# Four token rows of a PEER layer, copied eight times in HBM before they are given out to 128 partitions

## The chip, the cores and the metric

The kernel runs on one core of a Trainium2 chip. The metric is the time of one execution on the device in microseconds (us). A core has a matrix engine (TensorE, PE in the profile, with its weight loads as PEld), a vector engine (VectorE, DVE), a scalar engine (ScalarE, ACT), a general engine (GpSimd, POOL) and an engine that mostly issues DMAs (SyncE, SP). Sixteen DMA engines move data between the chip's memory (HBM) and the on-chip memory (SBUF, 128 partitions), whichever engine issues the transfer.

## The reference

One decoder layer on 256 tokens of width 2048, in float32: two kinds of attention, a normalization, a PEER layer, a normalization, a gated embedding, a normalization. The change lies in the PEER layer, which looks up 8 x 16 = 128 experts of 16384 for each token, and adds up their outputs:

```python
def block(args):
    xb, eb, gb = args              # tokens, chosen experts, gates
    ub = u[eb]                     # rows of peer_u, 2048 wide
    vbk = v[eb]                    # rows of peer_v
    act = jax.nn.gelu(jnp.einsum('thed,td->the', ub, xb).astype(jnp.float32))
    w = (gb * act).astype(xb.dtype)
    return jnp.einsum('the,thed->td', w, vbk)
```

`peer_u` and `peer_v` have 16384 rows of 8 KB, 134 MB each.

## The kernel before

**Stages.** Attention and the first normalization fill the first 415 us or so. Then follow the query (16 blocks of `peer_wq`, function `query`), 128 blocks of `peer_u` (`u_block`), 256 half blocks of `peer_v` (`v_block`), and the second normalization with the gate. Blocks of weights are loaded by SP with `su.load` (line 97) into `wf`, which has `WF = 5` buffers; a load is issued when PE has finished with the buffer.

**Two ways to the same sum.** The last 156 tokens (`NDT`) are computed densely: all 16384 activations by matmuls against the whole of `peer_u` (line 206, results through ACT in line 942, one activation per block), multiplied by gates that are zero but for the chosen experts (`gate_work`, whose small matmuls are lines 903 and 904 and whose scaling on DVE is line 913), then matmuls against `peer_v` (line 992). The first 100 tokens (`NSP`) are computed sparsely, by the function `sparse_work`: the rows of their chosen experts are gathered from HBM, 128 at a time, one for each partition, by an indirect DMA that POOL issues (line 851); DVE multiplies each gathered row by its token's x and sums (line 824); later the same goes for `peer_v`.

**Groups of tokens.** The sparse tokens are in three groups, `GROUPS = ((0, 64), (64, 32), (96, 4))`. The 128 partitions are shared out among the tokens of a group: in the first group each token has 2 partitions and 64 gathers are needed, in the second 4 partitions and 32 gathers, in the third 32 partitions and 4 gathers. So each partition needs the x of its token, and this is the tile `xq{i}`, a megabyte, made by the function `tokens` (line 803). It reads the tokens' rows of `s_x1` from HBM, repeated by an access pattern with a step of zero: 64 rows each twice, 32 rows each four times, 4 rows each 32 times. The first two are issued when `sparse_work` starts, the third (`xq2`) at the ninth gather of the second group. It takes over the buffer of `xq0`.

**Where x comes from.** The tensor `s_x1` is in HBM. In the query stage a background job, `spill_x1`, applies the last step of the normalization to x on POOL (lines 576 and 577) and writes it there in two DMAs of a megabyte (line 586), the first for tokens 0 to 127.

**Order.** SP, POOL and ACT each issue their DMAs in program order. The gathers are spread out: `gathers(n)` lets n of them out per block (1.8 per query block, 0.7 per block of `peer_u`, 0.35 per half block of `peer_v`), and each is held on POOL by a little copy (`pace`, line 849) until a 4-byte DMA on SP's queue (`mark`, line 848) has landed behind the loads before it. Four buffers (`NGB`) hold gathered rows. `keep` marks instructions that the scheduler leaves in program order.

Of the kernel before, what the change touches and what calls it, by code (L numbers as in the profile page):

```python
# [9 lines left out]
F32 = mybir.dt.float32  # L10
# [9 lines left out]
P = 128  # L20
T = 256
NT = T // P
D = 2048
# [16 lines left out]
SEG2 = NIA - SEG1  # L40

GROUPS = ((0, 64), (64, 32), (96, 4))
NSP = sum(n for _, n in GROUPS)
NDT = T - NSP
SELB = 8
# [110 lines left out]
def build(tc, a, out):  # L156
    nc = tc.nc
# [286 lines left out]
    x1 = [x1p.tile([P, D], F32, name=f"x1_{t}") for t in range(NT)]  # L444
# [68 lines left out]
    def ln_rows(pool, which):  # L513
        gr = pool.tile([P, D], F32, name="g_row", tag="g_row")
        br = pool.tile([P, D], F32, name="b_row", tag="b_row")
        load(gr, a["ln_g"][which:which + 1, :].to_broadcast([P, D]))
        load(br, a["ln_b"][which:which + 1, :].to_broadcast([P, D]))
        return gr, br
# [55 lines left out]
    def affine(xt, c, gr, br):  # L574
        s = slice(c * 512, (c + 1) * 512)
        nc.gpsimd.tensor_tensor(xt[:, s], xt[:, s], gr[:, s], op=ALU.mult)
        nc.gpsimd.tensor_tensor(xt[:, s], xt[:, s], br[:, s], op=ALU.add)

    def spill_x1():
        gr, br = ln_rows(rowp, 0)  # L580
        yield 4
        for t in range(NT):
            for c in range(NCH):
                affine(x1[t], c, gr, br)
                yield 10 if t else 4
            nc.gpsimd.dma_start(a["s_x1"][t * P:(t + 1) * P, :], x1[t])


    gin = pools.open("gin", "left", bufs=1)
# [8 lines left out]
    sel, eig, eact, ew = [], [], [], []  # L598
    for i, (_, n) in enumerate(GROUPS):
        sel.append(gin.tile([P, n], F32, name=f"sel{i}"))  # L600
# [98 lines left out]
    def gates(t):  # L699
# [12 lines left out]
        if t == 0:  # L712
            nc.vector.tensor_copy(eg[:NSP, 1].bitcast(F32), g[:NSP])
            for i in range(len(GROUPS)):
                slots(i, 1, by_slot(i, 1))
# [5 lines left out]
    def slots(i, w, src):  # L721

        t0, n = GROUPS[i]
        nc.gpsimd.dma_start(eig[i][:, w],
                            src[t0:t0 + n].rearrange("t (r j) -> t r j", j=n))

    def by_slot(i, w):

        t0, n = GROUPS[i]
        src = eg[t0:t0 + n, w].bitcast(F32)  # L730
        if n < PH:
            return eg[:, w].rearrange("t h k -> t (h k)")
        dst = es[t0:t0 + n, w].bitcast(F32)
        nc.vector.tensor_copy(dst.rearrange("t (r h c) -> t h r c", h=PH, r=P // n),
                              src.rearrange("t h (r c) -> t h r c", r=P // n))
        return es[:, w]

    def head_slots(h):

        c = slice(h * TOPK, (h + 1) * TOPK)  # L740
        nc.vector.scalar_tensor_tensor(eg[:NSP, 0, h], iaN[:NSP, 0, c], float(NKEY),
                                       ibN[:NSP, 0, c], op0=ALU.mult, op1=ALU.add)
        t0, n = GROUPS[0]
        m = n // PH
# [50 lines left out]
    def sparse_work():  # L795


        xq = []

        def tokens(i):  # L800
            t0, n = GROUPS[i]
            xq.append(gin.tile([P, D], F32, name=f"xq{i}", tag=f"xq{i % 2}"))
            nc.gpsimd.dma_start(xq[i], a["s_x1"][t0:t0 + n, None, :].to_broadcast([n, P // n, D]))

        tokens(0)
        tokens(1)
        made = []

        dots, acts = [], []

        def advance():

            if acts and gated:
                i, b = acts.pop(0)
                keep(nc.vector.tensor_tensor(ew[i][:, b], ew[i][:, b],
                                             eig[i][:, 1, b].bitcast(F32), op=ALU.mult))
            if dots:
                i, b = dots.pop(0)
                keep(nc.scalar.activation(ew[i][:, b], eact[i][:, b], AF.Gelu_apprx_tanh))
                acts.append((i, b))  # L820

        def use(kind, i, j, g):
            if kind == "u_rows":
                keep(nc.vector.scalar_tensor_tensor(g, g, 1.0, xq[i], op0=ALU.mult, op1=ALU.mult,  # L824
                                                    accum_out=eact[i][:, j:j + 1]))
            elif j == 0:
                if i < 2:
                    ys[i] = gin.tile([P, D], F32, name=f"y{i}", tag=f"xq{i}")
                else:

                    ys[i] = g
                keep(nc.vector.tensor_scalar(ys[i], g, ew[i][:, j:j + 1], None, op0=ALU.mult))
            else:
                keep(nc.vector.scalar_tensor_tensor(ys[i], g, ew[i][:, j:j + 1], ys[i],  # L834
                                                    op0=ALU.mult, op1=ALU.add))
            if j % SELB == SELB - 1 or j == GROUPS[i][1] - 1:
                advance()
                if kind == "u_rows":
                    dots.append((i, slice(j - j % SELB, j + 1)))

        for kind in ("u_rows", "v_rows"):
            for i, (_, n) in enumerate(GROUPS):
                for j in range(n):
                    if kind == "u_rows" and (i, j) == (1, 2 * NGB):
                        tokens(2)

                    mark = gin.tile([1, 1], F32, name="mark", tag="mark", bufs=32)
                    keep(nc.sync.dma_start(mark, a["c_iota"][0:1, 0:1]))
                    keep(nc.gpsimd.tensor_copy(pace, mark))  # L849
                    g = gin.tile([P, D], F32, name="gb", tag="gb", bufs=NGB)  # L850
                    keep(nc.gpsimd.indirect_dma_start(  # L851
                        out=g, out_offset=None, in_=a[kind],
                        in_offset=bass.IndirectOffsetOnAxis(ap=eig[i][:, 0, j:j + 1], axis=0)))
                    made.append((kind, i, j, g))
                    if len(made) >= NGB:
                        use(*made.pop(0))
                    yield
        while made:
            use(*made.pop(0))
# [14 lines left out]
    def gate_work(oh, parts, s0, ns, group):  # L874
# [32 lines left out]
        def scale(t0, n, ps):  # L907
            g = ps[:, :n * ns].rearrange("p (t a) -> p a t", t=n)
            c0 = 0
            for At in parts:  # L910
                dst = At[:, :, t0 - NSP:t0 - NSP + n]
                c1 = c0 + At.shape[1]
# [4 lines left out]
        made, multiplied = [], None  # L917
        for t0 in list(range(NSP, T, group)) + [None] * OHB:
            if t0 is not None:
# [29 lines left out]
    work = topk_work()  # L949
    sparse = sparse_work()  # L950
    bg.add(spill_x1(), 4)
    for hh in range(2 * PH):
        query(hh)
# [346 lines left out]
```

## Time and profile before

| | us |
|---|---|
| median of 3 runs | 1837.9 |
| lowest and highest of them | 1837.72, 1841.86 |
| the profiled execution, its own time | 1840.73 |
| its span, first to last instruction | 1838.9 |

| engine | busy us | share of the span |
|---|---|---|
| PE | 1775.4 | 97% |
| DVE | 1059.0 | 58% |
| POOL | 558.4 | 30% |
| ACT | 540.0 | 29% |

The DMA engines moved 608.78 MB, 331 GB/s on the mean. How to read the profile: "slices" are 40 equal parts of the span, with busy shares in tenths, the granted clock of TensorE in tenths of full speed, and the rate of the DMA engines. A row of a window gives its limits in us, its length, the busy time and instructions of each engine, then the granted clock, the DMA share and the rate. A row of the order of time gives start, duration, engine, line, operation, output and input, and in brackets the idle time before it and what ended it. A row of waits gives who waited for whom, the sum in us, the times and the longest. In a row of instructions "a/b/c" is least, median and greatest duration in ns, and "x18" a count.

### The profile page before, as it was taken

How to read it: one execution, taken by the hardware profiler on the slowest of the kernel's cores; microseconds unless marked ns; L12 is line 12 of the kernel's file. 1: busy time of each engine (PE TensorE's matmuls, PEld its weight loads, DVE VectorE, ACT ScalarE, POOL GpSimd, SP SyncE). 2: the span in 40 equal slices, each digit the busy share in tenths (PEclk: the TensorE clock that was granted, in tenths of full speed). 3: DMA queues.
4: the chain of work that ended last, by engine and by line, in shares of the span. 5: the costliest groups of instructions: out<-in, count | busy, mean ns of one | idle time of the engine just before them, and what ended most of it. 6: DMA issues, size and time to landing. Idle time of an engine off the chain costs nothing.

```text
span 1838.9 us, 30382 instructions
## 1 busy us (share of the span) xinstructions
PE 1775.4 (97%) x12110; PEld 1663.2 (90%) x12110; DVE 1059.0 (58%) x1659; ACT 540.0 (29%) x1351; POOL 558.4 (30%) x580
## 2 busy tenths in 40 slices
PE   8999999999999899997999999999999999998986
PEld 6888888888899899997899999999999999998766
DVE  5555688654898984442646545674434343333786
ACT  5687477632111001012333414550000000001532
POOL 0233133005563262321223323223233223231241
PEclk9999999999999999999999999999999999999998
DMA  7555645657999999999999999999999999998461
GB/s 276 192 164 163 234 142 160 247 202 280 361 368 416 415 417 420 420 386 302 386 379 405 406 398 406 374 390 375 419 420 421 419 420 416 421 420 343 146 260 52
DMA packets 99966, 608.78 MB, mean 331 GB/s; under 512 B 13144, under 2 KB 14992, under 8 KB 35696
## 3 DMA queue, kind: packets, MB, share of 16 engines
q1 hardware_dynamic: 66784, 384.24, 54.2%
q0 software_dynamic: 31312, 218.01, 29.7%
q10 hardware_dynamic: 1728, 4.59, 0.6%
q8 instruction: 95, 1.56, 0.3%
q14 instruction: 47, 0.39, 0.1%
HBM read 600.40 MB, written 6.29 MB: 330 GB/s over the span
## 4 chain that ended last, share of the span: by engine, by line
PE 81%; DMA 15%; DVE 3%; ACT 1%; issue 0%; SPq 0%; DVEq 0%; POOL 0%; ACTq 0%; POOLq 0%
PE ps_v L992 26%; PE ps_u L206 21%; DMA wf<-peer_u 7%; PE ps_qk L195 7%; PE ps_q L206 6%; PE ps_qk L197 3%; DMA wf<-peer_v 3%; DMA gb<-u_rows,eig 2%; PE ps_v L214 2%; PE ps_v L215 2%; PE ps_v L213 2%; PE ps_mix L213 1%; PE ps_mix L215 1%; PE ps_mix L214 1%; PE ps_gate L214 1%; PE ps_gate L215 1%
## 5 line engine op out<-in xcount | busy, mean ns | idle before, releaser
L206 PE MATMUL ps_u<-XF,wf 128*128 128x156 f32 x4096 | 561.9, 299 | 24.1 <-DMA wf<-peer_u 23.0
L206 PEld LDWEIGHTS ps_u<-XF,wf 128*128 128x128 f32 x4096 | 550.0, 191 | 30.1 <-DMA wf<-peer_u 16.8
L992 PE MATMUL ps_v<-A,wf 128*128 128x156 f32 x4096 | 553.5, 297 | 6.3 <-DMA wf<-peer_v 6.3
L992 PEld LDWEIGHTS ps_v<-A,wf 128*128 128x128 f32 x4096 | 545.9, 190 | 8.5 <-DMA wf<-peer_v 8.0
L834 DVE SCALAR_TENSOR_TENSOR y<-gb,ew,y 128x2048 f32<-128x2048 f32 x94 | 221.0, 2351 | 257.2 <-DMA gb<-v_rows,eig 254.5
L824 DVE SCALAR_TENSOR_TENSOR gb<-gb,xq 128x2048 f32<-128x2048 f32 x100 | 229.0, 2296 | 184.2 <-DMA gb<-u_rows,eig 184.1
L108 DVE TENSOR_TENSOR wl<-wf,wh 128x1024 fp32r<-128x1024 f32 (+1 forms) x201 | 222.7, 1132 | 114.1 <-ACT wh L107 112.3
L849 POOL COPY pace<-mark 1x1 f32<-1x1 f32 x200 | 111.7, 559 | 570.1 <-DMA mark<-c_iota 569.4
L107 ACT CAST wh<-wf 128x1024 fp32r<-128x1024 f32 (+1 forms) x201 | 173.0, 889 | 360.8 <-DMA wf<-ple_gate 250.7
L195 PE MATMUL ps_qk<-X,wh 128*128 128x512 f32 x512 | 185.2, 401 | 0.0
L942 ACT ACTIVATE A<-ps_u 128x156 f32<-128x156 f32 x128 | 38.3, 300 | 463.6 <-PE ps_u L206 364.7
L851 POOL DMA_INDIRECT gb<-u_rows,eig x100 | 127.0, 1270 | 140.5 <-DVE gb L824 79.2
L851 POOL DMA_INDIRECT gb<-v_rows,eig x100 | 136.3, 1363 | 53.6 <-issue 28.6
L197 PE MATMUL ps_qk<-X,wl 128*128 128x256 f32 x512 | 145.7, 285 | 0.0
L895 ACT ACTIVATE hi<-eq,ghf 128x64 f16<-128x64 f16 x312 | 104.4, 335 | 40.5 <-DVE eq L889 39.1
L195 PEld LDWEIGHTS ps_qk<-X,wh 128*128 128x128 f32 x512 | 96.4, 188 | 22.0 <-issue 1.0
L206 PE MATMUL ps_q<-XF,wf 128*128 128x256 f32 x512 | 113.6, 379 | 0.4 <-ACT eb L550 0.4
L206 PEld LDWEIGHTS ps_q<-XF,wf 128*128 128x128 f32 x512 | 95.9, 190 | 13.0 <-ACT eb L550 0.7
L896 ACT ACTIVATE lo<-eq,glf 128x64 f16<-128x64 f16 x312 | 104.1, 334 | 0.0
L197 PEld LDWEIGHTS ps_qk<-X,wl 128*128 128x128 f32 x512 | 96.3, 188 | 2.5 <-issue 1.3
L1011 ACT COPY XF<-ps_v 128x312 f32<-128x312 f32 x8 | 3.3, 418 | 188.2 <-PE ps_v L992 187.9
L214 PE MATMUL ps_gate<-wl,X 128*128 128x512 f32 (+1 forms) x144 | 53.8, 376 | 4.8 <-DVE wl L108 4.6
(240 smaller groups left out, 1767.2 us busy)
## 6 DMA issues: line engine op xcount, KB each, us to landing
wf<-peer_u SPq DMA_DIRECT2D x128, 1024.0 KB
wf<-peer_v SPq DMA_DIRECT2D x128, 1024.0 KB
wf<-w_qk SPq DMA_DIRECT2D x64, 512.0 KB
wf<-w_out SPq DMA_DIRECT2D x32, 512.0 KB
wf<-peer_wq SPq DMA_DIRECT2D x16, 1024.0 KB
wf<-ple_gate SPq DMA_DIRECT2D x16, 1024.0 KB
wf<-w_v SPq DMA_DIRECT2D x31, 512.0 KB
mark<-c_iota SPq DMA_DIRECT2D x200, 0.0 KB
```

Of the source, the lines that this page charges most:

```text
L107: self.order(nc.scalar.copy(wh, src))
L108: self.order(nc.vector.tensor_tensor(wl, src, wh.bitcast(F32), op=ALU.subtract))
L195: nc.tensor.matmul(ps, wh[:, j * P:(j + 1) * P], xt[:, dt, :], start=dt == 0, stop=False)
L197: nc.tensor.matmul(ps[:, :T], wl[:, j * P:(j + 1) * P], xt[:, dt, :T], start=False, stop=dt == ND - 1)
L206: nc.tensor.matmul(ps[:, :T - t0], wf[:, dt * P:(dt + 1) * P], xt[:, dt, t0:], start=dt == 0, stop=dt == ND - 1)
L214: nc.tensor.matmul(ps, hi, wl, start=False, stop=False)
L824: keep(nc.vector.scalar_tensor_tensor(g, g, 1.0, xq[i], op0=ALU.mult, op1=ALU.mult, accum_out=eact[i][:, j:j + 1]))
L834: keep(nc.vector.scalar_tensor_tensor(ys[i], g, ew[i][:, j:j + 1], ys[i], op0=ALU.mult, op1=ALU.add))
L849: keep(nc.gpsimd.tensor_copy(pace, mark))
L851: keep(nc.gpsimd.indirect_dma_start(out=g, out_offset=None, in_=a[kind], in_offset=bass.IndirectOffsetOnAxis(ap=eig[i][:, 0, j:j + 1], axi ...
L895: nc.scalar.mul(hi[:, j, :], eq[:, j, :], ghf[:, t])
L992: return nc.tensor.matmul(ps[:, (j % 2) * NDT:(j % 2 + 1) * NDT], vf[:, j * P:(j + 1) * P], W_of(ia), start=False, stop=ia == NIA - 1 and ...
```

## The change

The background job writes the four rows of the third group a second time, eight times each, to a new tensor `s_xc` of 32 rows, straight from SBUF, between the two writes of `s_x1`. The third group's `xq2` is then read from these 32 rows, each four times, in place of four rows each 32 times. The values that reach `xq2` are the same.

```diff
+NCOPY = 8
...
             nc.gpsimd.dma_start(a["s_x1"][t * P:(t + 1) * P, :], x1[t])
+            if t == 0:
+                t0, n = GROUPS[2]
+                nc.gpsimd.dma_start(a["s_xc"], x1[0][t0:t0 + n, None, :].to_broadcast([n, NCOPY, D]))
...
         def tokens(i):
             t0, n = GROUPS[i]
             xq.append(gin.tile([P, D], F32, name=f"xq{i}", tag=f"xq{i % 2}"))
-            nc.gpsimd.dma_start(xq[i], a["s_x1"][t0:t0 + n, None, :].to_broadcast([n, P // n, D]))
+            src = a["s_x1"][t0:t0 + n]
+            if i == 2:
+                src, n = a["s_xc"].rearrange("t c d -> (t c) d"), n * NCOPY
+            nc.gpsimd.dma_start(xq[i], src[:, None, :].to_broadcast([n, P // n, D]))
...
             aps["s_x1"] = dram.tile([T, D], F32, name="s_x1")
+            aps["s_xc"] = dram.tile([GROUPS[2][1], NCOPY, D], F32, name="s_xc")
```

## The prediction

> **What bounds the kernel now.** I read the slices of the page first, then windows around the dip that they show, then the waits and the order of time in that place. From the page: the span, the slices of PE, its granted clock, DMA and rate.
>
> ```profile
> span 1838.9 us, 30382 instructions
> ...
> PE   8999999999999899997999999999999999998986
> ...
> PEclk9999999999999999999999999999999999999998
> DMA  7555645657999999999999999999999999998461
> GB/s 276 192 164 163 234 142 160 247 202 280 361 368 416 415 417 420 420 386 302 386 379 405 406 398 406 374 390 375 419 420 421 419 420 416 421 420 343 146 260 52
> ```
>
> TensorE is busy nearly throughout, and from slice 12 on the DMA engines are busy throughout as well, at 416 to 420 GB/s. Slice 18 (827 to 873 us) is the exception: the DMA share is still 9, the rate only 302, and PE falls to 7. A transfer is keeping engines busy while moving little. The order of time around it, on POOL and then PE (start, duration, engine, line):
>
> ```profile
> 808.08 0.96 POOL L851 DMA_INDIRECT gb<-u_rows,eig  x1 [0.56 <-issue]
> 809.04 0.76 POOL L803 DMA_DIRECT2D xq<-s_x  x1
> ...
> 825.01 6.18 PE L206 MATMUL ps_u<-XF,wf 128*128 128x156 f32 x32 [0.35 <-DMA wf<-peer_u]
> ...
> 834.52 6.18 PE L206 MATMUL ps_u<-XF,wf 128*128 128x156 f32 x32 [3.33 <-DMA wf<-peer_u]
> ...
> 843.79 4.51 PE L206 MATMUL ps_u<-XF,wf 128*128 128x156 f32 x32 [2.82 <-DMA wf<-peer_u]
> ...
> 853.00 6.16 PE L206 MATMUL ps_u<-XF,wf 128*128 128x156 f32 x32 [4.71 <-DMA wf<-peer_u]
> ```
>
> The issue at 809.04 is the load of `xq2`, the read that the change replaces. It queues behind a gather, and the trouble begins some 8 us later. Windows (PE busy, PEld, DVE, ACT, POOL, granted clock, DMA share, GB/s):
>
> ```profile
> 800.00:816.54 16.54, 16.51 (x125) 16.23 (x123) 9.36 (x12) 0.90 (x3) 3.34 (x5) 1.00 1.01 421
> 818.00:850.00 32.00, 22.69 (x143) 20.74 (x141) 3.53 (x4) 10.71 (x44) 3.60 (x7) 0.89 1.02 241
> 852.00:858.00 6.00, 5.00 (x25) 5.00 (x26) 0.20 (x1) 0.00 (x0) 0.00 (x0) 0.72 1.01 421
> 816.54:864.10 47.56, 34.75 (x232) 32.56 (x232) 9.36 (x11) 13.90 (x57) 4.74 (x9) 0.89 1.01 283
> 864.10:924.97 60.87, 55.34 (x455) 53.91 (x456) 40.61 (x54) 19.61 (x80) 17.04 (x19) 1.00 0.98 379
> 929.35:1058.92 129.57, 129.57 (x1104) 128.88 (x1100) 71.38 (x94) 49.40 (x202) 42.05 (x42) 1.00 1.00 398
> 816.54:924.97 108.43, 90.10 (x687) 86.47 (x688) 49.97 (x64) 33.52 (x137) 21.77 (x28) 0.95 0.99 337
> ```
>
> 421 GB/s before, 241 during, 421 after: the rate falls and comes back within a few us, at a full DMA share all along. PE also loses clock (0.89): the 32 matmuls of three of the four blocks above take 6.16 or 6.18 us, those of the other 4.51. The waits from 800 to 900 us (total, times, longest) show who suffers: the gathers as well as the weights.
>
> ```profile
> DVE gb L824 <- DMA gb<-u_rows,eig: 57.2, 12, 32.4
> ...
> PE ps_u L206 <- DMA wf<-peer_u: 13.1, 6, 4.7
> ```
>
> Why blame this load and not the gathers or the start of `gate_work`, which fall in the same place? Because its two sisters are in the trace. `xq0` (64 rows, each read twice) and `xq1` (32 rows, each read four times) move the same megabyte each, from the same tensor, on the same queue:
>
> ```profile
> 442.02 1.15 POOL L803 DMA_DIRECT2D xq<-s_x  x2 [7.44 <-DVE s L635]
> ...
> 446.68 0.59 POOL L745 DMA_DIRECT2D eig<-eg  x1 [1.02 <-DVE eg L741]
> ...
> 454.59 1.06 POOL L851 DMA_INDIRECT gb<-u_rows,eig  x1 [7.33 <-DMA eig<-eg]
> ...
> 447.00:453.00 6.00, 6.00 (x32) 5.33 (x31) 0.65 (x3) 0.69 (x2) 0.26 (x1) 1.00 1.01 414
> ```
>
> The small `eig` transfer is queued behind both and has landed when the gather of 454.59 goes out, and the rate in between is 414 GB/s. So 32 places read four times each go at full speed. What is peculiar to `xq2` is that it reads four rows 32 times each.
>
> **The change, part by part.**
>
> *The read.* After the change `xq2` is read as 32 rows of 8 KB, lying one after the other, each four times: the shape of `xq1`'s read exactly. Its price: at least 1.05 MB / 420 GB/s = 2.5 us of the DMA engines. At most: the old read took from about 818 to 852 us, 34 us for four places. If the limit is one per place, eight times as many places need 34 / 8 = 4.3 us. I take 2.5, since `xq1` is the nearest row. The DMA engines are full at that point (421 GB/s), so nothing hides it: it is part of the sum below.
>
> *What the stall costs now.* Each block of `peer_u` ends in one activation on ACT (L942), a clock of the stage:
>
> ```profile
> 816.54 0.30 ACT L942 ACTIVATE A<-ps_u 128x156 f32<-128x156 f32 x1 [4.01 <-PE ps_u L206]
> ...
> 924.97 0.30 ACT L942 ACTIVATE A<-ps_u 128x156 f32<-128x156 f32 x1 [3.01 <-PE ps_G L904]
> ...
> L942 ACT ACTIVATE A<-ps_u x18: 277/300/301, 816.5 to 920.0; 128x156 f32<-128x156 f32 x18
> ...
> L942 ACT ACTIVATE A<-ps_u 128x156 f32<-128x156 f32 x29 | 8.7, 300 | 81.6 <-PE ps_u L206 41.5 <-PE ps_G L903 24.7 <-PE ps_G L904 15.4
> ...
> L851 POOL DMA_INDIRECT gb<-u_rows,eig x14: 957/962/2582, 823.3 to 920.8; - x14
> ```
>
> 18 blocks take 108.43 us from 816.54 to 924.97. (Beyond 864 us the loads are still catching up: PE 55.34 of 60.87.) What would they take without the stall? Three ways:
> - By PE's pace with the same `gate_work` beside it: 29 blocks in 129.57 us (929.35 to 1058.92), all PE, is 4.47 us a block, and 18 are 80.4 us.
> - By DMA: 18 loads, 14 gathers and the new read of a megabyte each are 33 x 1.05 MB = 34.6 MB, at 420 GB/s 82.4 us.
> - By taking away what PE lost: 108.43 - 90.10 = 18.3 us idle, and (1 - 0.89) x 47.56 = 5.2 us of clock, leave 84.9 us. This still holds a few us in which the first products of `gate_work` wait for ACT.
>
> I take 83.0 us, a little above the DMA's bound: a gain of 25.4 us. Ends: 28.0 (the pace of PE alone) and 18.0, if the 5.5 us of idle PE after 864 us are the start of `gate_work` (84.9 + 5.5 = 90.4). With 1.8 us more for a limit per place the low end is 16.2.
>
> All of it should come off the end. From 929 us on PE waits for nothing (129.57 of 129.57), and what follows is timed by PE's blocks: the gathers are let out per block, and the later loads when a buffer is freed. Late next, where the stall goes, is PE itself, with the DMA engines close behind (398 to 420 GB/s).
>
> *The write.* One more DMA on POOL's queue, between the two writes of `s_x1`; its source is four partitions, each given out eight times, 0.26 MB. No instruction of another engine is added or moved, and the order on POOL is otherwise the same. POOL's issue costs what its neighbours do:
>
> ```profile
> 433.48 1.10 POOL L586 DMA_DIRECT2D s_x<-x  x2
> ```
>
> That is 0.55 us. The transfer is 0.6 us at 420 GB/s; at the pace of the old read (1.05 MB in 34 us) it is 8.5 us. Queued behind it are the second write of `s_x1`, then `xq0` and `xq1`, which wait for both writes, then `eig` and the first gather: all move by what it takes. What hides it: PE works on `peer_wq` blocks and has no wait in this stage (window 447 to 453: 6.00 of 6.00), and the DMA engines are free here and there up to slice 11 (361 and 368 GB/s). Where the cover ends, the gathers that start late are paid for at full DMA engines, from about 600 us. Below nothing it cannot be, for nobody waits less. I take 1 us, nearer to the row at full speed because `s_x1`'s own writes are; ends 0 and 8.5.
>
> The Trainium skill (DMA: Bandwidth & Descriptors, Why a DMA increments its semaphore by 16 and not by 1) says that a DMA uses as many of the 16 engines, at most, as divide the outermost size of both sides. By it the old read (outermost 4) ran on four engines, the new one (32) runs on 16, and the write (4 partitions) on four: 2.5 us as an estimate instead of 0.6, and the sum would be 1.9 us higher. The trace neither proves nor refutes it; the forecast of the read is the same by four engines as by four places.
>
> *The sum.* 25.4 - 1.0 = 24.4 us. The profiled execution took 1840.73 us (span 1838.9); less 24.4 this is 1816.3. It stands 2.8 us above the median of the runs, 1837.9, so in terms of that median I predict 1813.5 us.
>
> **The rivals.**
> 1. *The read stays partly slow.* 32 places are still too few when the other traffic is 421 GB/s of 1 MB loads and gathers; `xq1` was read beside lighter loads. For it: the load of the stage differs. Against it: the rate around `xq1` was 414, so the engines were as full. If half of the stall stays, 12.7 us go: 1826.
> 2. *No gain.* The dip belongs to the gathers or to the first products of `gate_work`, and the load only happens to be there. Against it: the gathers run before 816 us at 421 GB/s, and `gate_work` runs on at 398 with PE full. Then 1838 to 1839 with the write.
> 3. *Slower.* The write from four partitions holds up POOL's queue, so that `xq0`, the first gathers and all behind them start late, and the backlog is paid at full DMA engines. To end on the other side it must cost PE more than the 25.4 us saved and 5.5 us (0.3%): some 31 us, 3.6 times what the worst row of the trace gives (8.5). Then 1844 or more.
>
> **How the numbers follow.** 0.3% of 1838 is 5.5 us, about what these runs can tell from no change. The main case 0.82, with its own range 1808 to 1820 (gains of 28 and 18, and 2 us of scatter up and down); rival 1 0.10 (1820 to 1832); rival 2 0.05 (mostly within 0.3%); rival 3 0.03. The range reaches from 1808 up to 1823, into rival 1 and the dearer writes. Faster: 0.82 + 0.10 + 0.01 of rival 2 = 0.93; same 0.04; slower 0.03.
>
> **What would show it.** Right: no slice under 370 GB/s between 600 and 1100 us; in the 20 us behind the issue of `xq2` the rate stays near 420 with PE over 95% busy at clock 1.0; 18 blocks from there take 81 to 85 us; the longest wait of DVE for a gather drops from 32.4 us to under 10. The write: the first gather leaves at 455 to 458 us, and PE's waits for `peer_u` before 800 us grow by less than 2 us. Wrong: a dip at the same load although it has 32 places, or one in another place, at the write or where the gathers catch up.

## The result and the profile after

| | us |
|---|---|
| before, median of 5 runs | 1837.9 (1833.3 to 1841.86) |
| after, median of 5 runs | 1824.46 (1821.72 to 1826.05) |
| ratio, with its 95% interval | 0.9925 [0.9904, 0.9945] |
| the profiled execution of after, its own time | 1825.47 |

The change makes the kernel 13.4 us faster. The prediction was 1813.5 us with a range from 1808 to 1823: the direction is right, the gain is little more than half of what was forecast, and the time lies just above the range. From the page of after: the span, the slices of PE, its granted clock, DMA and rate.

```profile
span 1823.7 us, 30383 instructions
...
PE   8999999999998999999999999999999999999986
...
PEclk9999999999999999999999999999999999998999
DMA  7544644657899999999999999999999999997461
GB/s 281 189 167 162 231 147 155 234 204 263 310 376 415 415 420 419 421 420 420 411 401 406 399 404 407 371 379 387 420 420 420 419 418 417 421 420 330 155 256 52
```

The dip of slice 18 is gone: the rate there is 420 GB/s (302 before). But slice 10 (456 to 502 us) fell from 361 to 310. Windows of after: the first row is the 20 us behind the issue of the new `xq2` (at 817.60; it lands 14.8 us later), the second 32 us from the next block on, the third the same 18 blocks as before (the columns are those of the prediction's windows). Then DVE's waits for gathers from 800 to 900 us:

```profile
817.60:837.60 20.00, 18.89 (x127) 17.75 (x126) 8.20 (x11) 8.14 (x34) 4.90 (x7) 0.91 1.01 421
...
824.00:856.00 32.00, 30.89 (x246) 29.65 (x245) 17.35 (x21) 14.09 (x58) 6.93 (x10) 0.95 1.01 420
...
824.27:909.19 84.92, 83.81 (x687) 82.29 (x686) 48.02 (x59) 33.31 (x137) 21.80 (x28) 0.98 1.01 415
...
DVE gb L832 <- DMA gb<-u_rows,eig: 44.2, 15, 6.1
```

PE is busy for 97% of the 32 us, and the 18 blocks take 84.92 us in place of 108.43: 23.5 us gained. They start at 824.27, though, where they started at 816.54 before. Something ahead of the read costs 7.7 us, and, as the first of the 128 blocks ends 0.95 us earlier than before (539.52 against 540.47), 8.7 us in all. The profiled execution of after should so take 1840.73 - 0.95 + 8.7 - 23.5 = 1825.0 us; it took 1825.47, and what follows the last block of `peer_u` is 0.6 us longer in it.

The new write is where it begins. POOL's order of time in after, and the waits of PE and ACT that follow (start, duration, engine, line; idle time before it and what ended it):

```profile
433.13 0.56 POOL L588 DMA_DIRECT2D s_x<-x  x1
433.69 0.62 POOL L591 DMA_DIRECT2D s_xc<-x  x1
434.31 0.57 POOL L588 DMA_DIRECT2D s_x<-x  x1
440.03 1.14 POOL L811 DMA_DIRECT2D xq<-s_x  x2 [5.15 <-DVE CV L637]
...
468.57 1.05 POOL L859 DMA_INDIRECT gb<-u_rows,eig  x1 [22.45 <-DMA wf<-peer_wq]
...
588.69 0.31 ACT L711 ACTIVATE gate<-gate 128x128 f32<-128x128 f32 x1 [22.17 <-DVE gate L707]
590.42 0.86 ACT L950 ACTIVATE A<-ps_u 128x156 f32<-128x156 f32 x4
...
590.76 70.83 PE L208 MATMUL ps_u<-XF,wf 128*128 128x156 f32 x512 [8.92 <-ACT A L950]
```

POOL issues everything in time; the transfers land late. The DMA issues of after, with the median us from issue to landing as the last figure:

```profile
s_x<-x POOLq DMA_DIRECT2D x2, 1024.0 KB, 14.6
xq<-s_x POOLq DMA_DIRECT2D x2, 1024.0 KB, 24.3
...
s_xc<-x POOLq DMA_DIRECT2D x1, 256.0 KB, 19.0
```

A quarter of a megabyte takes 19.0 us, and the two loads behind it 24.3. In a run without this write (e10, below) the same rows are

```profile
s_x<-x POOLq DMA_DIRECT2D x2, 1024.0 KB, 7.4
xq<-s_x POOLq DMA_DIRECT2D x2, 1024.0 KB, 10.6
```

So the first gather leaves at 468.57, 14 us after that of before (454.59). (The row names a load of `peer_wq` as what ended its wait, but the gather needs its indices: `eig`, issued at 445.52, landed after 22.2 us, where it took 7.6 in before.) DVE works through the gathers late. Its gates are late too, and ACT, which works in program order, waits 22.17 us for them with the activations of finished blocks queued behind: PE stops for 8.92 us at 590.76. That is the conspicuous place; it isn't where the time is lost for good. Windows of before over 48 blocks and the six after them,

```profile
540.47:756.72 216.25, 208.12 (x1544) 204.70 (x1543) 160.59 (x375) 21.32 (x62) 88.50 (x107) 1.00 1.01 418
756.72:782.16 25.44, 25.44 (x194) 25.44 (x193) 10.83 (x10) 1.90 (x8) 4.91 (x7) 1.00 1.02 421
```

and of after over the same blocks:

```profile
539.52:758.36 218.84, 208.04 (x1542) 206.63 (x1540) 170.24 (x404) 21.14 (x61) 90.09 (x112) 0.98 1.01 418
758.36:789.61 31.25, 26.91 (x193) 25.82 (x194) 14.64 (x14) 1.91 (x8) 8.46 (x12) 1.00 1.02 421
```

Over the 48 blocks that hold PE's stop, after loses only 2.6 us: before has idle time there as well, for the DMA engines set the pace (418 GB/s in both). The next six take 5.8 us longer, at full DMA engines (421), with PE waiting for weights. I read this as bytes that were not moved earlier, and the count of them agrees. Windows of before over the 50 us around the write and over the whole stage up to 757 us,

```profile
430.00:480.00 50.00, 50.00 (x247) 44.40 (x246) 31.56 (x120) 5.21 (x14) 20.32 (x28) 1.00 0.84 325
430.00:757.00 327.00, 318.87 (x2101) 303.63 (x2100) 246.50 (x645) 34.65 (x95) 147.62 (x171) 1.00 0.97 392
```

and of after:

```profile
430.00:480.00 50.00, 50.00 (x247) 44.40 (x246) 18.61 (x77) 5.22 (x14) 15.02 (x25) 1.00 0.78 271
430.00:757.00 327.00, 316.23 (x2085) 303.34 (x2084) 243.72 (x643) 34.21 (x94) 138.74 (x168) 0.98 0.96 385
```

Around the write 50 us x (325 - 271) GB/s = 2.7 MB are not moved, which at 420 GB/s is 6.4 us of full engines; up to 757 us it is 327 x (392 - 385) = 2.3 MB, 5.5 us. The same window has 392 to 394 GB/s in the runs whose write is cheap or missing (e1, e2, e4, e5, e6, e10) and 383 to 387 in those that write from four neighbouring partitions at this place (e3, e7, e8, e11).

### The profile page after: what moved, and what is told of

Same layout as the page of the kernel before. It is cut to its first block, busy times and chain, and to the rows that moved or that the text cites. A ratio compares the mean times of both kernels' runs of the same rounds, so it can differ in the third digit from the quotient of the medians.

```text
span 1823.7 us, 30383 instructions
## 1 busy us (share of the span) xinstructions
PE 1772.4 (97%) x12110; PEld 1663.8 (91%) x12110; DVE 1058.7 (58%) x1659; ACT 540.0 (30%) x1351; POOL 548.6 (30%) x581
## 4 chain that ended last, share of the span: by engine, by line
PE 85%; DMA 9%; DVE 4%; ACT 1%; issue 1%; POOL 0%; SPq 0%; DVEq 0%; ACTq 0%; POOLq 0%
PE ps_v L1000 27%; PE ps_u L208 25%; PE ps_qk L197 7%; PE ps_q L208 6%; DMA wf<-peer_u 4%; DMA wf<-peer_v 4%; PE ps_qk L199 3%; PE ps_v L216 2%; PE ps_v L217 2%; PE ps_mix L215 2%; PE ps_mix L216 2%; PE ps_mix L217 2%; PE ps_v L215 2%; DVE wl L110 1%; DMA gb<-u_rows,eig 1%; PE ps_gate L216 1%
## 5 line engine op out<-in xcount | busy, mean ns | idle before, releaser
L857 POOL COPY pace<-mark 1x1 f32<-1x1 f32 x200 | 107.2, 536 | 564.5 <-DMA mark<-c_iota 564.1
L859 POOL DMA_INDIRECT gb<-v_rows,eig x100 | 130.9, 1309 | 54.7 <-issue 32.2
```

The lines of the kernel that those rows point to most:

```text
L859: keep(nc.gpsimd.indirect_dma_start(out=g, out_offset=None, in_=a[kind], in_offset=bass.IndirectOffsetOnAxis(ap=eig[i][:, 0, j:j + 1], axi ...
```

## The experiments

Two questions. What made the old read slow: its four places, or that its outermost size is 4? And what does the write cost, and through what? All times are medians, with ratios to the kernel before on the same chip (1838.75 us in the first set, 1839.3 in the second, 1838.93 in the third).

**e1, the read in four transfers, and no write.** Each of the four rows is read in a transfer of its own, into 32 partitions: four places still, but the outermost size of each transfer is 32.

```diff
-            nc.gpsimd.dma_start(xq[i], a["s_x1"][t0:t0 + n, None, :].to_broadcast([n, P // n, D]))
+            if i == 2:
+                for k in range(n):
+                    nc.gpsimd.dma_start(xq[i][k * P // n:(k + 1) * P // n],
+                                        a["s_x1"][t0 + k:t0 + k + 1, :].to_broadcast([P // n, D]))
+                return
```

> The kernel before, with the read of xq2 cut into four DMAs, one per token: each reads one row 32 times into 32 partitions. Still four places in HBM and no copies, but the outermost size of each DMA is 32, not 4. If four places are what makes the read slow, the stall stays: 1838 us, 18 blocks behind the load in some 108 us, the rate near 240 GB/s. If it is that an outermost size of 4 puts the whole megabyte on four of the sixteen DMA engines, the stall goes: 18 blocks in 85 us as in the changed kernel, and 1838 - 23.5 = 1814 us, since no write is paid for.

Measured: 1820.49 us, ratio 0.9907 [0.9886, 0.9927]. Without any copy the time is 18.3 us under before and below that of the change. The 18 blocks take 85.2 us, as was expected; the expected time, 1814, was too low by 6 us (why is said below).

**e2, 128 places, outermost size 4.** `xq2` is read from 128 different rows by one transfer whose outermost size is still 4. The values are other rows of x.

```diff
+            if i == 2:
+                nc.gpsimd.dma_start(xq[i], a["s_x1"][0:P].rearrange("(c t) d -> t c d", t=n))
+                return
```

> The kernel before, with xq2 read from 128 different rows of the first half of x, none of them twice, but in an order that keeps the outermost size at 4 (partition 32t + c takes row 4c + t). The third group so gets the x of other tokens, and its four output rows are wrong; the work is the same. If places count, 128 of them are as good as any load: the stall goes, 1814 us. If the outermost size of 4 counts, all is as before: 1838 us, the rate near 240 GB/s for some 34 us.

Measured: 1839.08 us, ratio 1.0007 [0.9996, 1.0018]. The window of e2 over the read:

```profile
818.00:850.00 32.00, 22.21 (x143) 20.46 (x141) 3.53 (x4) 10.41 (x43) 3.60 (x7) 0.89 1.02 246
```

The same window of e1, whose read has the four places of before:

```profile
818.00:850.00 32.00, 30.89 (x246) 29.65 (x245) 14.16 (x18) 13.71 (x56) 7.47 (x10) 0.95 1.02 371
```

246 GB/s with 128 places, 371 with four. The number of places isn't the cause of the stall.

**e6, outermost size 8.** This is the kernel before with eight rows read 16 times each (other rows of x for half of the partitions).

```diff
+            n = 8 if i == 2 else n
```

> The kernel before, with xq2 read from eight rows, each 16 times, in place of four rows each 32 times: outermost size 8, no write. Four rows of the eight are other tokens', so the third group's output differs. If the outermost size is the number of DMA engines, eight engines carry 16 rows each where four carried 32: over an even share of 8 rows, a surplus of 8 in place of 24. The stall shrinks to a third or so and the time is about 1838.7 - 2/3 x 18.5 = 1826 us; the low rate lasts some 10 to 15 us. If only 16 engines help, it stays near 1838; if anything above four is enough, 1820 us.

Measured: 1827.26 us, ratio 0.9944 [0.9927, 0.9961]. Its window:

```profile
818.00:850.00 32.00, 25.84 (x207) 24.05 (x206) 8.37 (x9) 11.42 (x48) 6.54 (x8) 1.00 1.02 305
```

The dip has about half its depth (305, between 246 and 371) and about two thirds of the gain is there. The Trainium skill (DMA: Bandwidth & Descriptors, Why a DMA increments its semaphore by 16 and not by 1) says that a DMA uses, at most, as many of the 16 engines as divide the outermost size of both sides. By it 4, 8 and 32 are four, eight and sixteen engines, and the three runs agree: 1839.08, 1827.26 and 1820.49 us. No view here names the engine that carried a packet, so the runs show the dependence on the outermost size, and the engines are the Trainium skill's reading of it.

**e3, the write alone.** The change with the old read; the copies are written and nobody reads them.

```diff
-            src = a["s_x1"][t0:t0 + n]
-            if i == 2:
-                src, n = a["s_xc"].rearrange("t c d -> (t c) d"), n * NCOPY
-            nc.gpsimd.dma_start(xq[i], src[:, None, :].to_broadcast([n, P // n, D]))
+            nc.gpsimd.dma_start(xq[i], a["s_x1"][t0:t0 + n, None, :].to_broadcast([n, P // n, D]))
```

> The changed kernel's write of the copies, which nobody reads: xq2 is read from four rows as before. If the write is what took back the gain, this is slower than before by the 8.7 us by which the changed kernel's blocks had fallen behind when xq2 was loaded: 1846.6 us, with the first gather near 468 us and the pause of PE near 582 to 590 us. If the write is hidden and the loss has another cause, 1838 us.

Measured: 1845.79 us, ratio 1.0042 [1.0026, 1.0058]. The write costs 7.0 us. The first gather leaves at 467.71, and PE waits 8.2 us for ACT's activation, as in the change.

**e4, the same bytes from 32 partitions.** (The 32 rows are those of 32 tokens.)

```diff
-                nc.gpsimd.dma_start(a["s_xc"], x1[0][t0:t0 + n, None, :].to_broadcast([n, NCOPY, D]))
+                nc.gpsimd.dma_start(a["s_xc"].rearrange("t c d -> (t c) d"), x1[0][64:96, :])
```

> The changed kernel, but the 32 rows of s_xc are written from 32 partitions (tokens 64 to 95, once each) in place of four partitions eight times each; same bytes, same place in the queue. The third group so gets the x of other tokens, and its four output rows are wrong. If the write is slow for its four source partitions, it now lands within 7 us, the first gather leaves at 455 to 457 us, and the whole read gain is seen: 1814 us. If any write at this place costs as much, 1824.5 us as in the changed kernel.

Measured: 1819.71 us, ratio 0.9897 [0.9881, 0.9914]. POOL's order of time in e4:

```profile
453.59 1.06 POOL L859 DMA_INDIRECT gb<-u_rows,eig  x1 [8.64 <-DMA mark<-c_iota]
```

The first gather leaves as early as in before. The same number of bytes, at the same place in POOL's queue, costs nothing that can be measured.

**e5, four partitions that are eight apart.** Partitions 64, 72, 80 and 88 (other tokens' rows); all else as in the change, the outermost size of 4 too.

```diff
-                nc.gpsimd.dma_start(a["s_xc"], x1[0][t0:t0 + n, None, :].to_broadcast([n, NCOPY, D]))
+                nc.gpsimd.dma_start(a["s_xc"], x1[0][64:96:8, None, :].to_broadcast([n, NCOPY, D]))
```

> The changed kernel, with the copies written from four partitions that lie apart (64, 72, 80 and 88, each eight times) in place of the neighbours 96 to 99. Four source partitions and an outermost size of 4, as in the change; the third group gets the x of other tokens, so its output rows differ. If the write is slow because neighbouring partitions share one way out of SBUF, its packets now take some 0.3 us each, the write lands within 8 us and the time is that of the write from 32 partitions, 1820 us. If it is slow because four engines each read one partition again and again, the write lands after some 19 us as before, and the time is 1824.5 us.

Measured: 1819.15 us, ratio 0.989 [0.9873, 0.9908]. Its DMA issues:

```profile
xq<-s_x POOLq DMA_DIRECT2D x2, 1024.0 KB, 14.6
...
s_xc<-x POOLq DMA_DIRECT2D x1, 256.0 KB, 10.2
```

The landing, 10.2 us, is a little over what was expected (8); the cost is gone. So neither the write's outermost size nor the eightfold reading of each row is what makes it dear.

**e7, the change once more**, in one set with e5.

> The changed kernel once more, on the same chip as the three beside it. 1824.5 us as before; some 4 to 5 us above the kernel with the write from 32 partitions and the one with four reads (1819.7 and 1820.5 us).

Measured: 1825.76 us, ratio 0.9926 [0.991, 0.9943]; the write landed after 19.0 us again, and the first gather left at 468.83. Against e5 the four neighbouring partitions cost 6.6 us.

**e11, four other neighbours.** Partitions 64 to 67.

```diff
-                nc.gpsimd.dma_start(a["s_xc"], x1[0][t0:t0 + n, None, :].to_broadcast([n, NCOPY, D]))
+                nc.gpsimd.dma_start(a["s_xc"], x1[0][64:68, None, :].to_broadcast([n, NCOPY, D]))
```

> As the change, but the copies are written from the four neighbouring partitions 64 to 67 in place of 96 to 99 (xq2 then holds the x of other tokens). Theory 'neighbours': what makes the write slow is that its four source partitions lie side by side; it lands in 17 to 20 us, and the time is that of the change, 1824 to 1827. Rival 'these partitions': something else about 96 to 99 is slow; then it lands in about 10 us, as from partitions eight apart, and the time is 1818 to 1821.

Measured: 1825.37 us, ratio 0.9929 [0.9907, 0.9951].

```profile
s_xc<-x POOLq DMA_DIRECT2D x1, 256.0 KB, 18.3
```

18.3 us: the neighbours 64 to 67 are as slow as 96 to 99. The Trainium skill (SBUF — State Buffer, Door 1: The DMA port swizzle) says that partitions 64 to 67 and 96 to 99 share one of 16 ports for DMAs, while the ones of e5 lie on four ports. The runs agree with it (19.0 and 18.3 us against 10.2); they don't show the ports themselves, and as both groups lie on one port by it, no run tells whether four neighbours elsewhere are as slow.

**e8, the write on ACT's queue.** It was meant to go out at the ninth query block, some 50 us later.

```diff
-            if t == 0:
-                t0, n = GROUPS[2]
-                nc.gpsimd.dma_start(a["s_xc"], x1[0][t0:t0 + n, None, :].to_broadcast([n, NCOPY, D]))
...
+        if hh == 8:
+            t0, n = GROUPS[2]
+            nc.scalar.dma_start(a["s_xc"], x1[0][t0:t0 + n, None, :].to_broadcast([n, NCOPY, D]))
```

> The changed kernel, with the write of the copies issued from ACT after the ninth query block (some 50 us later) in place of from POOL between the writes of x. If the write costs by standing ahead of the reads of xq0 and xq1 and the first index transfer in POOL's queue, the cost is gone: first gather at 451 to 457 us, 1820 us. If it costs by holding four DMA engines for some 13 us wherever it stands, the gathers of that time wait instead, and part or all of it stays: 1822 to 1825 us.

Measured: 1826.65 us, ratio 0.9932 [0.9916, 0.9949]. The edit did not do what was meant. The scheduler moved the issue forward, as the order of time on ACT's queue in e8 shows:

```profile
432.65 1.23 ACTq L961 DMA_DIRECT2D s_xc<-x  x1
```

POOL's order of time in e8:

```profile
455.32 1.15 POOL L808 DMA_DIRECT2D xq<-s_x  x2 [20.45 <-DMA s_x<-x]
...
471.49 1.06 POOL L856 DMA_INDIRECT gb<-u_rows,eig  x1 [11.92 <-DMA eig<-eg]
```

So e8 tested another queue at the same time of issue. The write on ACT's queue holds up POOL's transfers as much: the writes of `s_x1` land late, and `xq0` waits 20.45 us for them. That the write stands in POOL's queue isn't the cause.

**e9, the write late indeed.** The same edit with the write inside `keep`, which holds it in program order.

> The write of the copies stands on ACT's queue and is held in program order, so that it goes out after the ninth query block (about 500 us) and not at 433 us. Theory 'place': the write costs 6 to 7 us only because the two loads xq0 and xq1 and the first transfer of indices stand behind it in the stage where they are already late; then the first gather leaves at 452 to 459 us and the time is that of the copies without the price, 1819 to 1821. Rival 'engines held': the write of four neighbouring partitions holds engines for 14 to 19 us wherever it stands, weights and gathers wait for it there, and the time is 1824 to 1827.

Measured: 1825.24 us, ratio 0.9931 [0.9911, 0.995]. This time it goes out at 483.08 us, and the first gather leaves at 451.61. POOL's order of time in e9:

```profile
451.61 1.06 POOL L856 DMA_INDIRECT gb<-u_rows,eig  x1 [5.87 <-DMA eig<-eg]
```

The order of time of ACT and its queue:

```profile
483.08 1.23 ACTq L961 DMA_DIRECT2D s_xc<-x  x1
...
582.99 0.31 ACT L708 ACTIVATE gate<-gate 128x128 f32<-128x128 f32 x1 [16.85 <-DVE gate L704]
```

The theory of the place fell. The head of POOL's queue is in time, and the time is still 4 to 6 us above e1, e4, e5 and e10: the gathers from 475 to 520 us are held up instead (15.3 us from issue to landing in the median, 9.5 in e10), ACT waits 16.85 us for its gates, and PE stops for 3.6 us. The window of e9 up to 757 us has 389 GB/s:

```profile
430.00:757.00 327.00, 317.85 (x2086) 303.00 (x2085) 246.22 (x644) 34.20 (x94) 137.80 (x169) 0.99 0.96 389
```

That is 3 GB/s under before, which is worth 327 x 3 / 420 = 2.3 us; it accounts for about half. Where the loss lies can be said: PE's 50th to 55th block of `peer_u` take 31.1 us, as in the change (31.25), against 26.5 in e10, with PE waiting for weights. What the rest of e9's cost comes from stays open.

**e10, e1 once more**, beside e9 and e11.

> The kernel before with xq2 read in four transfers, one for each token, without copies; once more, on the chip that also runs the variants of the write. If its advantage over the change is real, it is 1818 to 1822 again, 4 to 6 us below the change and 17 to 20 below the kernel before. If it was scatter of one chip, it is at 1823 or more.

Measured: 1821.25 us, ratio 0.9909 [0.9894, 0.9924]. Reading each token's row in a transfer of its own beats both kernels, and needs no copy: 17.7 us under before, and 4 us under e9 and e11, which write from four neighbours. (The copies with a cheap write, e4 and e5, are as fast, 1819.71 and 1819.15 us, but hold other tokens' rows.)

## Why the prediction was right or wrong, point by point

**The place and the cause of the stall: right.** The dip belongs to `xq2`'s read: e1, e4, e5 and the change remove it without touching the gathers or `gate_work`, so rival 2 falls. Rival 1 named a time (1826) close to the one measured, but for a read that stays half slow; the rate was 420 GB/s, so it falls too. "Places" as the cause, which the text used and called the same as four engines for this forecast, is refuted by e1 and e2.

**The new pace of the 18 blocks: nearly right.** They take 84.92 us instead of 83.0, within the 81 to 85 given. The value got by taking away what PE lost (84.9) came closest of the three, in part by luck: it took off all of the lost clock, and the granted clock is still 0.98 over the 18 blocks. One sign was missed by a little: in the 20 us behind the issue PE is busy for 94%, not over 95%, at a clock of 0.91, not 1.0, so a part of the lost clock there was not the stall's. DVE's longest wait for a gather fell to 6.1 us, as foretold. What was won stays to the end, as foretold too: the last 47 blocks of `peer_u` take 207.3 us in both kernels.

**The gain of the read in terms of the median: too high.** It is 23.5 us over the 18 blocks of the two profiled executions, but 18 to 20 by medians: e1 18.3, e10 17.7, e4 19.0, e5 20.1. The failed step is that 25.4 was taken from one execution, whose stall was long. From the same block on, the 18 blocks took 105.25 us in e2 and 102.2 in e3, which have the same read, against 108.43. And before had come to its stall sooner than e2: the 62 blocks ahead of it took 276.1 us against 278.1. From the activation of the first block to that of the 81st the traces agree better: 384.5 us in before and 383.3 in e2, against 363.4 to 363.9 in e1, e4, e5 and e10, some 20 us for the read, as by medians. The sum then also took off 2.8 us for the profiled execution being slower than the median, although the long stall is probably a part of why it was (e2's execution was 3.6 us shorter, its stall 3.2): some of the same us were counted twice. Smaller slips don't bear on this: the rate behind slice 12 is not 416 to 420 GB/s throughout but 374 to 406 in slices 19 to 27 of before, and gains of 28 and 18 with 2 us of scatter give 1808 to 1822 for the main case, not to 1820.

**The write: the mechanism was named, the size was wrong.** The step that failed is "I take 1 us, nearer to the row at full speed because `s_x1`'s own writes are". Those go out from 128 partitions, this one from four neighbours, and it landed after 19.0 us; even the upper end of 8.5 us was too short for the transfer, though not for its cost in medians (7.0 by e3, 6.6 by e7 against e5). The 8.7 us of the two profiled executions are too much, since before came early to its stall; up to the 81st block the change, e7, e8 and e11 take 369.3 to 370.0 us, some 6 us over e1, e4, e5 and e10. (e3's profiled execution, the fastest of its seven, is only 1 to 2 us over before and e2 there.) This step put the time outside the range: with 1 us for the write, the read's 18 to 20 us would have ended at 1819 to 1821. The cover was misjudged as well: PE had indeed no wait in this stage, but the free DMA time that was named as cover is what the write used up, 325 GB/s down to 271, and the bytes owed came due around 760 to 790 us. The first gather left at 468.57, not at 455 to 458. PE's waits for `peer_u` from 540 to 816 us even fell (6.2 us against 7.7), as the forecast allowed; the wait that appeared, for ACT's activation behind a late gate, was not foreseen. This is rival 3's chain of events, at some 7 us instead of the 31 it needed to decide the sign.

**The estimate of 2.5 us for the write.** The prediction worked it out from the four engines that such a write gets by the Trainium skill (DMA: Bandwidth & Descriptors, Why a DMA increments its semaphore by 16 and not by 1). An outermost size of 4 isn't what makes the write dear: e5, which has the same outermost size of 4, costs nothing that can be measured. Its landing took 10.2 us beside the other traffic, so the 2.5 us themselves are neither shown nor refuted.

**The sum with the terms as measured:** a read of 17.7 to 20.1 us and a write of 6.6 to 7.0 give 10.7 to 13.5 us of gain, 1824.4 to 1827.2 from 1837.9; measured 1824.46.

## What to carry to other kernels

Look at the outermost size of a transfer's access pattern before blaming the memory: a megabyte with an outermost 4 slowed everything for 34 us, and four transfers with 32 each cured it without a copy. A transfer is not hidden because the compute engine has no wait where it runs; if the DMA engines are full later, count the bytes that do not move while it is under way, and divide them by the full rate. And a stall that is read from one execution has the size of that execution: don't also subtract the distance of that execution from the median.

## What the runs showed of the hardware that was not expected

- A write of 256 KB from four neighbouring partitions, each read eight times, takes 19.0 us (18.3 from four others), from partitions eight apart 10.2 us, beside the same traffic. While it is under way the transfers of POOL's queue are late even when it is on ACT's queue: `s_x1`'s two writes landed after 23.1 us in e8, after 7.4 in e10.
- A transfer with an outermost size of 4 lowers the rate of all traffic, from 421 to 241 GB/s in before and to 246 in e2, at a full DMA share. In the packet records of before the 8 KB packets of SP's loads take 0.43 us in the median from 818 to 850 us, and 0.31 from 780 to 812. Why the whole slows down so far when only this transfer is lopsided was not settled.
- Rows read from four places cost little: in the window from 818 to 850 us e1 moved 371 GB/s and e4, with 32 places, 419, and their times are 1820.49 and 1819.71 us.
